# High and low x in one product for three retention projections, memory squares behind a weight cast, and earlier block scores

## The chip, the cores and the metric

The kernel runs on one core of one Trainium2 chip. The metric is device time in microseconds (us) of one execution; the median of three runs of the kernel before is 427.76 us (427.15 to 428.31). Engines are named as in the profile: PE (TensorE matmul), PEld (its weight load), DVE (VectorE), ACT (ScalarE), POOL (GpSimd), SP (SyncE, which issues nearly all transfers).

## The reference

A two-layer decoder trunk over 256 tokens of width 1024, followed by a final norm. Every layer normalises x, projects it to the columns of all its groups, gates each group's output with SiLU, maps the concatenation back with one output projection and adds it to x. Cut to what matters here:

```python
def even_layer(x, mem_n, ...):                      # layer 0
    h = rms_norm(x, norm_g)
    (nq, nkc, ..., mq, mk, mv, mz, eq, ez) = _split(h @ w_in, EVEN_SPLITS)
    a_out = nsa_attention(...)                      # sparse attention, 8 heads; compressed blocks need an MLP
    b_out = moba_attention(rot(mq), rot(mk), heads(mv))        # block attention, 8 heads
    m_out = memory_attention(heads(eq), mem_n, w_mem_kv)       # 4 heads into 256 memory tokens
    y = jnp.concatenate([a_out * silu(nz), b_out * silu(mz), m_out * silu(ez)], -1) @ w_out
    return x + y

def odd_layer(x, mem_n, ...):                       # layer 1
    h = rms_norm(x, norm_g)
    rq, rk, rv, rz, eq, ez = _split(h @ w_in, ODD_SPLITS)      # rq, rk: 4 heads x 256
    q = apply_rotary(rq...); k = apply_rotary(rk...) * (RET_QK_DIM ** -0.5)
    r_out = head_group_norm(retention(q, k, v))     # per head: (q k^T * decay) v + carried state
    m_out = memory_attention(eq..., mem_n, w_mem_kv)
    return x + jnp.concatenate([r_out * silu(rz), m_out * silu(ez)], -1) @ w_out
```

`mem_n` is the memory (256 rows of 1024) normalised by its rows' mean square.

## The kernel before, in words

**Products.** x, memory and every weight are split in two parts, high and low, each in the 32-bit type that the profile calls fp32r. A product is then three matmuls: high x by high weight, low x by high weight, high x by low weight (`mm3`, lines 245 to 247). Weights come in units of 128x1024: SP loads `raw`, ACT makes `whi` (line 166), DVE makes `wlo` = raw - whi (line 174). `whi` and `wlo` have four buffers each (`NB`), so a cast waits until the unit four before it is used up on the PE. A projection of 512 columns takes four units; a unit holds two of the eight row blocks kt for all 512 columns. Where tokens lie on the partitions of the result (`project`), the weight moves (512 columns); where the result is turned, with its 512 columns on partitions in four column tiles ct (`project_turned`), the weight tile is what is loaded and x moves, 256 columns at a time. There each bank of PSUM (128x512) holds two column tiles side by side. The high and low halves of x are two tiles with the tag `big`, four buffers in all; the same tag holds those of the memory, of layer 1's x and the outputs of retention heads 0 and 1.

**Stages.** Layer 0 projects group by group; beside it run the attention chains as generators (`couple`, one for each pair of head pairs): scores on the PE (line 116), maxima (DVE, line 580 causal), exponentials (ACT, line 593), scaling by the gate and the sum (DVE line 555, ACT line 553), transposes on the PE (line 324), copies from PSUM (ACT, line 611), products with the values (PE, line 116), and the SiLU gate (lines 652, 655, 657: `tmp`, then `y` or `ym` as high and low halves). There are four sparse pairs, then block pairs 0 and 1, then the memory attention, which reaches into the out-projection. The rows of the retention projections are called `rq0`, `rk0` (heads 0 and 1) and `rq1`, `rk1` (heads 2 and 3); each is turned, rotated (`ret_qk`, lines 1099 to 1101) and used by two heads.

**What sets the order.** The program is written as stages that yield; each yield of the running projection is a slot, and `turn` then lets every waiting chain do one step (`active`, `first`, `waiting`). `AT` holds slots before which certain steps may not come: "cmp" the compression's rotation and transposes (`compressed`, lines 739 and 740), "blk" its windows, "hid" its hidden layer. A chain takes banks from "s0", "s1", "t", "tr", "o" when they are free; while `crowded` is set, "tr" is not given out. Every engine then runs its instructions in the order in which they were emitted this way (`MANUAL`), SP's transfers included.

**Around the change.** `memory_scale` (generator started after the block values) loads the memory rows (`in_memtok`), squares and sums each row on ACT (line 418), works out the reciprocal root on DVE (`rs`, lines 421 and 132 to 137), and spreads it with two small matmuls (line 879). Its two squares stand between weight casts on ACT, and its DVE steps between the maxima of a sparse pair.

Of the kernel before, what the change touches and what calls it, by code (L numbers as in the profile page):

```python
# [33 lines left out]
AT = {"rows": 4, "rows1": 4, "spread": 12, "ret": 75, "nsa": 12, "cmp": 15, "blk": 18, "hid": 24}  # L34
# [27 lines left out]
def trunk(  # L62
# [165 lines left out]
    def pause(n):  # L228

        for _ in range(n):  # L230
            yield
# [6 lines left out]
    def making(task, *names):  # L238

        yield from task  # L240
        made.update(names)
# [42 lines left out]

    def project_mem(lhs):

        hi, lo = lhs
        ps = [bank("pj") for _ in range(2)]
        for k0 in range(0, KT, 2):
            wh, wl = unit()  # L290
            yield
            turned_unit(ps, lhs, wh, wl, (k0, k0 + 1), range(2))
            finish()
            yield
            for tok in range(2):
                for j in range(2):
                    kt = k0 + j
                    ts = slice(tok * P, (tok + 1) * P)
                    c = slice(j * 512 + 256, j * 512 + 512)
                    mm3(ps[1][:, tok * T : (tok + 1) * T], hi[:, kt, ts], lo[:, kt, ts], wh[:, c], wl[:, c],  # L300
                        kt == 0 and tok == 0, kt == KT - 1, True)
        return ps
# [57 lines left out]
    xh = tl("big", [P, KT, T], 4, F32R)  # L360
    xl = tl("big", [P, KT, T], 4, F32R)
# [195 lines left out]
    def couple(jobs, causal, products, close, name, need=None):  # L557

        spans, cols, blocks = (SPAN, 384, range(3)) if causal else (HALF, 512, (0, 2, 1, 3))
        tags = yield from take(4, FREE)  # L560
# [294 lines left out]
    def memory_rows():  # L855
        nonlocal mh, ml
        mh = tl("big", [P, KT, T], 4, F32R)
        ml = tl("big", [P, KT, T], 4, F32R)
# [9 lines left out]
    def memory_scale():  # L868
# [3 lines left out]
        yield  # L872
        yield from row_scale(mrow, rstdm, D)
        yield
# [52 lines left out]
    def block_couple(c):  # L927
# [4 lines left out]
        def products(o, pts):  # L932
            todo = []
            for i in range(2):
# [6 lines left out]
                          lambda o: making(gated(o, szb, yb, slice(2 * c, 2 * c + 2)), f"Yb{c}"), f"yb{c}")  # L941
# [37 lines left out]
    waiting.extend(({"mq", "mk", "mvt", "szb", f"yb{c - 1}" if c else "yn3"}, block_couple(c)) for c in range(2))  # L979
    drive(memory_queries())  # L980
    crowded = True
    drive(memory_keys())
# [61 lines left out]
    x1h = tl("big", [P, KT, T], 4, F32R)  # L1044
    x1l = tl("big", [P, KT, T], 4, F32R)
# [46 lines left out]
    def ret_qk(name):  # L1092

        both = tl("v4", [P, 2, 2, T], NV)
        ps = now(project_turned((x1h, x1l)))
        for i in range(2):
            pv = ps[i].rearrange("p (k t) -> p k t", k=2)
# [41 lines left out]
    for h in range(4):  # L1139
# [14 lines left out]
        y = tl("big", [P, 2, 4, T], 4, F32R) if h < 2 else tl("y", [P, 2, 4, T], 2, F32R)  # L1154
# [152 lines left out]
```

## Time and profile before

| what | before |
| --- | --- |
| median of 3 runs | 427.76 us (427.15 to 428.31) |
| the profiled execution, its own time | 427.74 us |
| its span | 425.9 us (1.84 us lie around it) |
| granted TensorE clock, mean | 0.999 |
| PE busy | 417.7 us, 98%, 2620 matmuls |
| DVE busy | 305.7 us, 72% |
| ACT busy | 245.6 us, 58% |
| chain that ended last | PE 92%, DVE 3%, DMA 3%, ACT 1% |

The page has one row per engine, groups of instructions by line, and the chain of work that ended last. Matmuls overlap one another, so one that lasts 0.28 us may follow its predecessor by 0.12 us; what counts on a full PE is the distance from start to start. In the rows of the timeline the columns are start, duration (both us), engine, line, operation, output and inputs, shape of the output and count; what stands in brackets is the engine's idle time before the row and what ended it. Line 319 (`rb`) and line 662 (`s<-pj,rstdm`) are copies of 128x256 from PSUM, by DVE and by ACT, in other places of the same kernel.

### The profile page before, as it was taken

To read this page: it belongs to the slowest core of one execution; us is meant where nothing else is said; L and a number is where in the kernel's file an instruction comes from. 1 tells how busy PE (TensorE), PEld (TensorE's weight loads), DVE (VectorE), ACT (ScalarE), POOL (GpSimd) and SP (SyncE) were. 2 spreads that over 40 slices of the span, in tenths; PEclk is the share of its full clock that TensorE was granted. 3 is DMA by queue.
4 is the path that set the end of the run, shared out by engine and by line. 5 is a ranking of instruction groups with operands and counts; after the bars stand their busy time and mean duration, and the time that the engine had idled before them with its cause. 6 is when DMAs were issued, how large, how long until landed. Compare 5 with 4: busy or idle time off the path is not lost.

```text
span 425.9 us, 7020 instructions
## 1 busy us (share of the span) xinstructions
PE 417.7 (98%) x2620; PEld 361.4 (85%) x2620; DVE 305.7 (72%) x675; ACT 245.6 (58%) x453; POOL 1.9 (0%) x9
## 2 busy tenths in 40 slices
PE   8999999999999999999999999999999999999994
PEld 6889987878889887779999988889998888888884
DVE  3878996977678577588578675677887467685545
ACT  4768476777777586755456344456444445545613
POOL 1000000000000000000000000000000000000000
PEclk9999999999999999999999999999999999999999
DMA  7997545254563852536445545546444555656202
GB/s 247 334 372 254 194 136 192 67 184 160 184 191 110 287 175 97 169 128 195 157 145 168 170 167 168 196 159 198 158 158 159 184 192 175 205 170 189 80 0 99
DMA packets 22801, 74.23 MB, mean 174 GB/s; under 512 B 2928, under 2 KB 4464, under 8 KB 22768
## 3 DMA queue, kind: packets, MB, share of 16 engines
q1 hardware_dynamic: 22192, 73.14, 52.2%
q10 hardware_dynamic: 576, 0.66, 0.6%
q8 instruction: 20, 0.33, 0.3%
q14 instruction: 13, 0.11, 0.1%
HBM read 72.73 MB, written 1.05 MB: 173 GB/s over the span
## 4 chain that ended last, share of the span: by engine, by line
PE 92%; DVE 3%; DMA 3%; ACT 1%; issue 0%; SPq 0%; DVEq 0%; ACTq 0%
PE pj L245 23%; PE pj L247 22%; PE pj L246 22%; PE o L116 3%; PE s L409 2%; PE s L324 2%; PE s L116 2%; PE t L324 1%; DMA raw<-in_w 1%; PE tr L245 1%; PE tr L247 1%; PE tr L246 1%; DMA raw<-in_memtok 1%; PE t L116 1%; PE s L246 1%; PE s L247 1%
## 5 line engine op out<-in xcount | busy, mean ns | idle before, releaser
L174 DVE TENSOR_TENSOR wlo<-raw,whi 128x1024 fp32r<-128x1024 f32 (+1 forms) x118 | 142.1, 1207 | 61.8 <-ACT whi L166 59.7
L166 ACT CAST whi<-raw 128x1024 fp32r<-128x1024 f32 (+1 forms) x118 | 121.7, 1036 | 88.4 <-PE pj L247 38.0
L245 PE MATMUL pj<-whi,big 128*128 128x512 f32 (+2 forms) x256 | 97.3, 383 | 0.0
L246 PE MATMUL pj<-wlo,big 128*128 128x512 f32 (+2 forms) x256 | 96.1, 376 | 0.0
L247 PE MATMUL pj<-whi,big 128*128 128x512 f32 (+2 forms) x256 | 95.8, 374 | 0.0
L245 PE MATMUL pj<-big,whi 128*128 128x256 f32 x256 | 73.6, 287 | 0.0
L247 PE MATMUL pj<-big,wlo 128*128 128x256 f32 x256 | 72.6, 284 | 0.0
L246 PE MATMUL pj<-big,whi 128*128 128x256 f32 x256 | 72.5, 283 | 0.0
L245 PEld LDWEIGHTS pj<-whi,big 128*128 128x128 f32 x256 | 48.2, 188 | 9.3 <-issue 1.5
L247 PEld LDWEIGHTS pj<-whi,big 128*128 128x128 f32 x256 | 48.2, 188 | 8.7
L246 PEld LDWEIGHTS pj<-wlo,big 128*128 128x128 f32 x256 | 48.3, 189 | 8.1 <-DVE wlo L174 0.4
L245 PEld LDWEIGHTS pj<-big,whi 128*128 128x128 f32 x256 | 49.0, 191 | 1.9 <-issue 1.8
L246 PEld LDWEIGHTS pj<-big,whi 128*128 128x128 f32 x256 | 49.0, 192 | 0.1
L247 PEld LDWEIGHTS pj<-big,wlo 128*128 128x128 f32 x256 | 49.0, 191 | 0.0
L593 ACT ACTIVATE p<-p,mx 128x128 f32<-128x128 f32 (+1 forms) x48 | 21.2, 443 | 5.3 <-DVE mx L580 5.3
L245 PE MATMUL pj<-whi,y 128*128 128x512 f32 x42 | 16.9, 407 | 0.0
L247 PE MATMUL pj<-whi,y 128*128 128x512 f32 x42 | 16.4, 390 | 0.0
L246 PE MATMUL pj<-wlo,y 128*128 128x512 f32 x42 | 16.3, 391 | 0.0
L555 DVE TENSOR_SCALAR p<-p,sm 128x256 f32<-128x256 f32 (+1 forms) x48 | 12.7, 322 | 0.6
L343 ACT ACTIVATE big<-raw,vec 128x256 fp32r<-128x256 f32 x16 | 7.7, 505 | 5.2 <-DMA vec<-in_vec 2.5
L553 ACT ACTIVATE p<-p,sm 128x256 f32<-128x256 f32 (+1 forms) x16 | 7.6, 484 | 4.9 <-DVE sm L549 4.0
L580 DVE CUSTOM_DVE_ANT_0 p<-s,cst 128x128 f32<-128x128 f32 (+1 forms) x24 | 7.1, 355 | 4.4 <-PE s L116 4.3
(349 smaller groups left out, 644.5 us busy)
## 6 DMA issues: line engine op xcount, KB each, us to landing
raw<-in_w SPq DMA_DIRECT2D x90, 512.0 KB, 3.9
raw<-in_wout SPq DMA_DIRECT2D x28, 512.0 KB, 4.1
v<-in_xtok SPq DMA_DIRECT2D x4, 512.0 KB, 6.4
raw<-in_w SPq DMA_DIRECT2D x4, 280.0 KB, 5.3
raw<-in_w SPq DMA_DIRECT2D x4, 256.0 KB, 6.2
v<-in_w SPq DMA_DIRECT2D x2, 512.0 KB, 7.5
raw<-in_memT SPq DMA_DIRECT2D x2, 512.0 KB, 4.2
raw<-in_memtok SPq DMA_DIRECT2D x2, 512.0 KB, 4.9
```

The source lines that it names most:

```text
L116: ins = PE.matmul(out, lhs, rhs, start=start, stop=stop)
L166: S.copy(hi, raw)
L174: V.tensor_tensor(lo, raw, hi.bitcast(F32), ALU.subtract)
L245: PE.matmul(ps, lh, rh, start=start, stop=False, skip_group_check=shared)
L246: PE.matmul(ps, lh, rl, start=False, stop=False, skip_group_check=shared)
L247: return PE.matmul(ps, ll, rh, start=False, stop=stop, skip_group_check=shared)
L324: PE.transpose(b[:, i * P : (i + 1) * P], a, ident)
L343: S.activation(hi[:, kt], raw[:, kt - k0], AF.Copy, scale=g[:, kt : kt + 1])
L409: PE.matmul(ps_k[tok], x[:, kt, tok * P : (tok + 1) * P], w, start=kt == 0 and i == 0, stop=kt == KT - 1 and i == 2)
L553: S.activation(p[:, hh, a], p[:, hh, a], AF.Copy, scale=sm[:, hh, tok : tok + 1])
L555: V.tensor_scalar(p[:, hh, a], p[:, hh, a], sm[:, hh, tok : tok + 1], None, op0=ALU.mult)
L593: S.activation(ps[i][:, hh, a], src, AF.Exp, bias=ms[i][:, hh, tok : tok + 1], scale=-1.0 if causal else 1.0, accum_out=ns[i][:, hh, tok : ...
```

## The change

Three things are done, and a few steps shift with them.

1. `project_paired` replaces `project_turned` for `rq0`, `rk0` and `rq1`, not for `rk1`. High and low x lie in one tile (`xp`, `mp`, `x1p`: 128 x 2 x 8 x 256), and one matmul moves both, 512 columns, against a high weight tile; a second one moves high x alone, 256 columns, against the low weight tile. The two results of the first stand side by side in a bank, so a projection takes four banks (three "pj" and "tr") where it took two, and `ret_qk` adds the halves: ACT copies the low half to SBUF (line 1119 of the kernel after), DVE adds the high half (line 1120), four times 128x256 each for a projection. The rotation then reads SBUF. `y01` holds the outputs of heads 0 and 1 in one tile, so that all uses of `big` have the new size (two buffers).
2. `memory_scale` waits two slots before the squares and three before the spread.
3. The block pairs no longer wait for the gate path `szb`; block pair 1 may take "tr", "s0", "s1", "t" for its scores; `crowded` is set only after the memory keys. "cmp" is 14 instead of 15 and "hid" 23 instead of 24.

The diff (in the kernel after, lines of `couple` and the rest of layer 0 stand 17 further down: 418 becomes 435, 555 becomes 572, 580 becomes 597, 611 becomes 628; those of `ret_qk` 25):

```diff
@@ -31,7 +31,7 @@
 BANKS = {"pj": 3, "tr": 1, "t": 1, "s0": 1, "s1": 1, "o": 1}
 FREE = ("s0", "s1", "t", "tr", "o")
 NEG = -1e30
-AT = {"rows": 4, "rows1": 4, "spread": 12, "ret": 75, "nsa": 12, "cmp": 15, "blk": 18, "hid": 24}
+AT = {"rows": 4, "rows1": 4, "spread": 12, "ret": 75, "nsa": 12, "cmp": 14, "blk": 18, "hid": 23}
 MAGIC = 12582912.0
 PI_LO = 3.1415925
 BASE = 16512 + 32 + 416 + 32
@@ -282,6 +282,23 @@
                 finish()
         return ps
 
+    def project_paired(pair):
+
+        ps = [bank(tag) for tag in ("pj", "pj", "pj", "tr")]
+        for kt in range(0, KT, 2):
+            wh, wl = unit()
+            for ct in range(4):
+                if ct % 2 == 0:
+                    yield
+                for j in range(2):
+                    c = slice(j * 512 + ct * P, j * 512 + ct * P + P)
+                    k = kt + j
+                    PE.matmul(ps[ct], wh[:, c], pair[:, :, k], start=k == 0, stop=False, skip_group_check=True)
+                    PE.matmul(ps[ct][:, :T], wl[:, c], pair[:, 0, k], start=False, stop=k == KT - 1, skip_group_check=True)
+                if ct % 2:
+                    finish()
+        return ps
+
     def project_mem(lhs):
 
         hi, lo = lhs
@@ -357,8 +374,8 @@
     G.memset(warm, 0.0)
     ident = cpak[:, C_ID : C_ID + P]
     xrow = [tl("v4", [P, D], NV) for _ in range(2)]
-    xh = tl("big", [P, KT, T], 4, F32R)
-    xl = tl("big", [P, KT, T], 4, F32R)
+    xp = tl("big", [P, 2, KT, T], 2, F32R)
+    xh, xl = xp[:, 0], xp[:, 1]
     ps_k = [bank(f"s{tok}") for tok in range(2)]
     xraw, wraw = [], []
     for q in range(4):
@@ -554,10 +571,10 @@
                 else:
                     V.tensor_scalar(p[:, hh, a], p[:, hh, a], sm[:, hh, tok : tok + 1], None, op0=ALU.mult)
 
-    def couple(jobs, causal, products, close, name, need=None):
+    def couple(jobs, causal, products, close, name, need=None, banks=FREE):
 
         spans, cols, blocks = (SPAN, 384, range(3)) if causal else (HALF, 512, (0, 2, 1, 3))
-        tags = yield from take(4, FREE)
+        tags = yield from take(4, banks)
         ss, todo = [], []
         for i, (q, k, gate) in enumerate(jobs):
             ss.append([bank(tag) for tag in tags[2 * i : 2 * i + 2]])
@@ -854,8 +871,8 @@
 
     def memory_rows():
         nonlocal mh, ml
-        mh = tl("big", [P, KT, T], 4, F32R)
-        ml = tl("big", [P, KT, T], 4, F32R)
+        mp = tl("big", [P, 2, KT, T], 2, F32R)
+        mh, ml = mp[:, 0], mp[:, 1]
         for q in range(2):
             mraw = load(tl("raw", [P, 1024], NRAW), memT[:, 4 * q : 4 * q + 4].rearrange("p k t -> p (k t)")).rearrange("p (k t) -> p k t", k=4)
             yield
@@ -869,9 +886,9 @@
         nonlocal rstdm, rbm
         mrow = [load(tl("raw", [P, 1024], NRAW), memtok[:, tok]) for tok in range(2)]
         rstdm = tl("rstdm", [P, 2])
-        yield
+        yield from pause(2)
         yield from row_scale(mrow, rstdm, D)
-        yield
+        yield from pause(3)
         rbm = tl("rbm", [P, T])
         tag, = yield from take()
         b = bank(tag)
@@ -938,7 +955,8 @@
             return todo
 
         yield from couple([(mq[:, 2 * c + i], mk[:, 2 * c + i], None) for i in range(2)], True, products,
-                          lambda o: making(gated(o, szb, yb, slice(2 * c, 2 * c + 2)), f"Yb{c}"), f"yb{c}")
+                          lambda o: making(gated(o, szb, yb, slice(2 * c, 2 * c + 2)), f"Yb{c}"), f"yb{c}",
+                          banks=("tr", "s0", "s1", "t") if c else FREE)
 
     def memory_keys1():
         nonlocal k1, v1m
@@ -976,10 +994,10 @@
     drive(block_values())
     active.append(making(memory_scale(), "rbm"))
     drive(block_gates())
-    waiting.extend(({"mq", "mk", "mvt", "szb", f"yb{c - 1}" if c else "yn3"}, block_couple(c)) for c in range(2))
+    waiting.extend(({"mq", "mk", "mvt", f"yb{c - 1}" if c else "yn3"}, block_couple(c)) for c in range(2))
     drive(memory_queries())
+    drive(memory_keys())
     crowded = True
-    drive(memory_keys())
 
 
     def part(acc, tok, c0, n, y, k, wh, wl, start, stop):
@@ -1041,8 +1059,8 @@
     strict = crowded = False
 
 
-    x1h = tl("big", [P, KT, T], 4, F32R)
-    x1l = tl("big", [P, KT, T], 4, F32R)
+    x1p = tl("big", [P, 2, KT, T], 2, F32R)
+    x1h, x1l = x1p[:, 0], x1p[:, 1]
     ss1 = tl("ss1", [P, 2, 2])
     rstd1 = tl("rstd1", [P, 2])
     rb1 = tl("rb", [P, T], 2)
@@ -1092,9 +1110,16 @@
     def ret_qk(name):
 
         both = tl("v4", [P, 2, 2, T], NV)
-        ps = now(project_turned((x1h, x1l)))
+        paired = name != "rk1"
+        ps = now(project_paired(x1p) if paired else project_turned((x1h, x1l)))
         for i in range(2):
-            pv = ps[i].rearrange("p (k t) -> p k t", k=2)
+            if paired:
+                pv = tl("rot_a", [P, 512], 2).rearrange("p (k t) -> p k t", k=2)
+                for k in range(2):
+                    S.copy(pv[:, k], ps[2 * i + k][:, T:])
+                    V.tensor_tensor(pv[:, k], ps[2 * i + k][:, :T], pv[:, k], ALU.add)
+            else:
+                pv = ps[i].rearrange("p (k t) -> p k t", k=2)
             b = tl("rot_b", [P, 512]).rearrange("p (k t) -> p k t", k=2)
             V.tensor_tensor(both[:, i], pv, ctr.unsqueeze(1).to_broadcast([P, 2, T]), ALU.mult)
             V.tensor_tensor(b, pv[:, ::-1, :], str_, ALU.mult)
@@ -1151,7 +1176,9 @@
         sz = tl("v4", [P, 2, 512], NV)
         for tok in range(2):
             S.activation(sz[:, tok], ps[tok], AF.Silu, scale=rstd1[:, tok : tok + 1])
-        y = tl("big", [P, 2, 4, T], 4, F32R) if h < 2 else tl("y", [P, 2, 4, T], 2, F32R)
+        if h == 0:
+            y01 = tl("big", [P, 2, 2, 4, T], 2, F32R)
+        y = y01[:, h] if h < 2 else tl("y", [P, 2, 4, T], 2, F32R)
         ret_head(h, qs[h % 2], kks[h % 2], vh, vl, sz, y)
         ys.append((y, 4, 6 + 2 * h, ()))
```

How instructions move, as each engine runs them (names carry the number under which their tile was made; `s` names are banks "s0", "s1" or SBUF tiles of the tag `s2`, `t`, `tr`, `o`, `pj` are banks).

ACT, around the squares of the memory rows, before (`raw_1257` and `raw_1259` are the memory rows, `whi` the weight casts, `pt` the copies of sparse pair 1's transposes, `y` and `p` the gate and exponentials behind):

```order
L611 COPY pt_1275<-o_1250 128x384
L418 ACTIVATE raw_1257,ss_1278<-raw_1257 128x1024
L166 CAST whi_1292<-raw_1083 128x1024
L418 ACTIVATE raw_1259,ss_1278<-raw_1259 128x1024
L166 CAST whi_1363<-raw_1141 128x1024
L655 CAST y_82<-tmp_275_1334 128x256
L593 ACTIVATE p_1336,sm_1338<-p_1336,mx_1337 128x128
```

and after:

```order
L628 COPY pt_1273<-o_1248 128x384
L166 CAST whi_1288<-raw_1081 128x1024
L435 ACTIVATE raw_1255,ss_1316<-raw_1255 128x1024
L435 ACTIVATE raw_1257,ss_1316<-raw_1257 128x1024
L166 CAST whi_1353<-raw_1139 128x1024
L672 CAST y_81<-tmp_273_1331 128x256
L610 ACTIVATE p_1333,sm_1335<-p_1333,mx_1334 128x128
```

The first weight cast now stands ahead of the first square, and the second one behind both. The six DVE steps of `rs` that follow the squares (lines 421 and 132 to 137) stood between the maxima of a sparse pair's two halves, and now stand behind both halves, ahead of the same `wlo` (line 174).

PE, the scores of block pair 1 (`v_173` are the keys and `v_210` the queries, in the kernel after `v_172` and `v_209`; `v_251` there are the values and `pt` the turned probabilities; the other rows are the memory keys' projection). Before, they stand alone between two units' matmuls, while the products of block pair 0 stand 24 matmuls ahead of them:

```order
L245 MATMUL pj_1677<-big_1058,whi_1679 128x256
L246 MATMUL pj_1677<-big_1059,whi_1679 128x256
L247 MATMUL pj_1677<-big_1058,wlo_1680 128x256
L116 MATMUL s_349_1796<-v_173_859,v_210_1033 128x128
L116 MATMUL s_350_1797<-v_173_859,v_210_1033 128x128
L116 MATMUL s_349_1796<-v_173_859,v_210_1033 128x256
L116 MATMUL s_350_1797<-v_173_859,v_210_1033 128x256
L116 MATMUL t_1798<-v_173_859,v_210_1033 128x128
L116 MATMUL o_1799<-v_173_859,v_210_1033 128x128
L116 MATMUL t_1798<-v_173_859,v_210_1033 128x256
L116 MATMUL o_1799<-v_173_859,v_210_1033 128x256
L245 MATMUL pj_1678<-whi_1679,big_1058 128x256
```

After, they follow the products of block pair 0 at once:

```order
L116 MATMUL o_1738<-pt_1690,v_251_1233 64x128 x2
L116 MATMUL o_1738<-pt_1717,v_251_1233 64x256 x2
L116 MATMUL o_1738<-pt_1717,v_251_1233 64x128 x2
L116 MATMUL tr_1747<-v_172_858,v_209_1032 128x128
L116 MATMUL s_344_1748<-v_172_858,v_209_1032 128x128
L116 MATMUL tr_1747<-v_172_858,v_209_1032 128x256
L116 MATMUL s_344_1748<-v_172_858,v_209_1032 128x256
L116 MATMUL s_345_1749<-v_172_858,v_209_1032 128x128
L116 MATMUL t_1750<-v_172_858,v_209_1032 128x128
L116 MATMUL s_345_1749<-v_172_858,v_209_1032 128x256
L116 MATMUL t_1750<-v_172_858,v_209_1032 128x256
L245 MATMUL pj_1683<-big_1057,whi_1638 128x256
```

One interruption of the projection remains of two. The same holds for the scores of block pair 0 and the products of sparse pair 3. What follows is earlier too: in the out-projection, the products of the memory attention stood 6 matmuls ahead of the first matmul that reads `ym`, and now stand 24 ahead of it.

PE, `rq0`, beginning behind scores of the memory attention, before (`big_2205` is high x, `big_2206` low x):

```order
L116 MATMUL t_2540<-s_462_2403,s_478_2530 128x256
L116 MATMUL tr_2541<-s_462_2403,s_478_2530 128x256
L245 MATMUL pj_2619<-big_2205,whi_2470 128x256
L246 MATMUL pj_2619<-big_2206,whi_2470 128x256
L247 MATMUL pj_2619<-big_2205,wlo_2471 128x256
```

and after, from the last column tile of `rq0` (bank `tr_2618`) to the first of `rk0` (banks `pj_2726` to `pj_2728`; `big_2203` holds both halves of x):

```order
L297 MATMUL tr_2618<-big_2203,wlo_2642 128x256
L296 MATMUL tr_2618<-big_2203,whi_2641 128x512
L296 MATMUL pj_2726<-big_2203,whi_2663 128x512
L296 MATMUL pj_2727<-big_2203,whi_2663 128x512
L296 MATMUL pj_2728<-big_2203,whi_2663 128x512
L297 MATMUL pj_2726<-big_2203,wlo_2664 128x256
```

A group of three matmuls over 256 columns became one over 512 and one over 256. The column tile that uses "tr" is left to the end of the projection in all four units, 16 matmuls in a row, of which the first two rows show two (a third, like the first of them, is left out behind them), since the memory attention, or the column tile "tr" of the projection before, still holds that bank; the next projection's first weight half can be cast only when the first of these units has been used there, and three matmuls by high weights stand ahead of the first by a low one.

## The prediction

> **What bounds the kernel now.** I read the page first, then a table of busy time by stretches, then the PE's list of waits.
>
> ```profile
> span 425.9 us, 7020 instructions
> PE 417.7 (98%) x2620; PEld 361.4 (85%) x2620; DVE 305.7 (72%) x675; ACT 245.6 (58%) x453; POOL 1.9 (0%) x9
> PE 92%; DVE 3%; DMA 3%; ACT 1%; issue 0%; SPq 0%; DVEq 0%; ACTq 0%
> ```
>
> The PE is busy for 98% of the span and carries 92% of the chain that ended last. A change pays only if it takes work, or a wait, off the PE. The stretches (PE, PEld, DVE, ACT, POOL busy, clock, DMA share, GB/s) tell where a wait is:
>
> ```profile
> 110.00:120.00 10.00, 8.84 (x73) 8.39 (x72) 9.55 (x43) 8.61 (x25) 0.00 (x0) 1.00 0.67 207
> 210.00:220.00 10.00, 10.00 (x84) 9.40 (x83) 7.08 (x9) 3.44 (x6) 0.00 (x0) 1.00 0.64 211
> 230.00:240.00 10.00, 10.00 (x86) 9.26 (x83) 8.11 (x11) 3.67 (x4) 0.00 (x0) 1.00 0.56 181
> ```
>
> At 110 to 120 us, in layer 0, the PE lacks 1.16 us while DVE is nearly full; at 210 to 240, where `rq0` and `rk0` are projected, it lacks nothing. The list of waits and the PE's own rows name the hole:
>
> ```profile
> PE s L324 <- DVE p L555: 1.2, 1, 1.2
> 115.86 0.28 PE L247 MATMUL pj<-big,wlo 128*128 128x256 f32 x1
> 117.29 0.92 PE L324 MATMUL s<-cst,p 128*128 128x128 f32 x5 [1.16 <-DVE p L555]
> ```
>
> From start to start this is 1.43 us where 0.12 is usual (below): 1.3 us are lost. The rows of ACT and DVE ahead of it say why:
>
> ```profile
> 107.71 1.06 ACT L418 ACTIVATE raw<-raw 128x1024 f32<-128x1024 f32 x1 [3.62 <-DMA raw<-in_memtok]
> 108.77 1.03 ACT L166 CAST whi<-raw 128x1024 fp32r<-128x1024 f32 x1
> 109.70 1.05 ACT L418 ACTIVATE raw<-raw 128x1024 f32<-128x1024 f32 x1
> 112.00 0.40 ACT L593 ACTIVATE p<-p,mx 128x128 f32<-128x128 f32 x1
> 109.83 1.23 DVE L174 TENSOR_TENSOR wlo<-raw,whi 128x1024 fp32r<-128x1024 f32 x1 [5.49 <-ACT whi L166]
> 110.97 0.42 DVE L652 TENSOR_TENSOR tmp<-o,v 128x256 f32<-128x256 f32 x1
> 112.41 0.17 DVE L421 TENSOR_SCALAR ss<-ss 128x2 f32<-128x2 f32 x1
> 113.41 0.16 DVE L137 SCALAR_TENSOR_TENSOR rstdm<-rs_t,rstdm 128x2 f32<-128x2 f32 x1
> 115.07 1.23 DVE L174 TENSOR_TENSOR wlo<-raw,whi 128x1024 fp32r<-128x1024 f32 x1
> 116.95 0.74 DVE L555 TENSOR_SCALAR p<-p,sm 128x128 f32<-128x128 f32 x3
> ```
>
> ACT sits for 3.62 us on a square whose memory rows have not landed; a weight cast is queued behind it; DVE idles 5.49 us for that cast and then has no pause until the probabilities `p` that the PE waits for.
>
> **The change, part by part.**
>
> *Memory squares behind the cast: −1.3 us.* The cast no longer needs the memory rows, so it runs inside ACT's 3.62 us, near 104.1 (107.71 less 3.62), its `wlo` and the first `tmp` before 107, and the maxima as their scores come. The rows still land at 107.7, so two squares end at about 109.75 (107.71 plus twice 1.0) and the second cast at 110.8, one cast (1.03) earlier than before relative to the exponentials: these start at about 111.0 rather than 112.00. The DVE steps on the squares take 1.2 us (112.41 to 113.41 and one more step), so they end at 111.0; the second `wlo` follows. From that `wlo` to the first `p` it was 1.88 us (115.07 to 116.95) and to the PE 2.22, so the PE could go at about 113.3.
>
> The last of the four blocks of `p` is scaled by ACT, behind all eight exponentials:
>
> ```profile
> L593 ACT ACTIVATE p<-p,mx 128x128 f32<-128x128 f32 (+1 forms) x48 | 21.2, 443 | 5.3 <-DVE mx L580 5.3
> L553 ACT ACTIVATE p<-p,sm 128x256 f32<-128x256 f32 (+1 forms) x16 | 7.6, 484 | 4.9 <-DVE sm L549 4.0
> ```
>
> 111.0 + 8 x 0.443 + 0.484 = 115.0. The PE arrives at 115.98 (115.86 + 0.12), or some tenths earlier by what is saved ahead. The cover is about 0.7 us, so I take the whole 1.3. If the squares held the exponentials as the cast did, nothing would be gained; so the bounds are 0 and −1.3. The spread behind them moves too, to a place beside no other work on the PE; its four DVE rows have been ready for long, and it costs a mode change (below).
>
> *Pairing: −1.15 us.* First and last rows of two even stretches, 75 steps of 256 columns and 11 of 512:
>
> ```profile
> 208.09 0.28 PE L245 MATMUL pj<-big,whi 128*128 128x256 f32 x1
> 217.09 0.28 PE L245 MATMUL pj<-big,whi 128*128 128x256 f32 x1
> 263.68 0.39 PE L245 MATMUL pj<-whi,big 128*128 128x512 f32 x1
> 266.18 0.39 PE L247 MATMUL pj<-whi,big 128*128 128x512 f32 x1
> ```
>
> That is 0.120 us for 256 columns and 0.227 for 512; so a matmul costs 0.013 us beside its columns (2 x 0.120 − 0.227). Each group drops one of them: 3 x 0.120 = 0.360 becomes 0.347. There are 3 projections x 32 groups = 96: 96 x 0.012 = 1.15 us off the path. No row alternates 512 and 256. Should the 0.013 sit in the weight load rather than in the matmul, the alternation would hide it wholly (0.107 for 256 columns and 0.214 for 512, 0.321 a group, −3.8 us in all); should a 512 behind a 256 pay for it twice, nothing would be saved (0). I take the constant, since 512 columns, with ample time for a load, show it as well.
>
> By the Trainium skill, "TensorE: Matmul & The Clock Gate", section "Back-to-back issue gap", a warm matmul takes 262 cycles for 256 columns and 518 for 512; my estimate from that page is 786 against 780 cycles a group, 0.24 us in all. The trace's 0.120 us is more than the 0.109 of 262 cycles at the page's 2.4 GHz, and 0.227 more than 0.216; the measured rows decide, and a sum by the page would end 0.9 us higher.
>
> *The additions of the halves: 0 to +0.6, taken as 0.1.* Per projection, four ACT copies and four DVE additions, and the rotation's six rows as before:
>
> ```profile
> L662 ACT ACTIVATE s<-pj,rstdm 128x256 f32<-128x256 f32 x4 | 1.7, 463 | 1.8 <-PE pj L247 1.8
> L1099 DVE TENSOR_TENSOR v<-pj,ctr 128x512 f32<-128x512 f32 x8 | 5.5, 683 | 0.0
> L174 DVE TENSOR_TENSOR wlo<-raw,whi 128x1024 fp32r<-128x1024 f32 (+1 forms) x118 | 142.1, 1207 | 61.8 <-ACT whi L166 59.7
> ```
>
> ACT gets 4 x 0.46 = 1.9 us more in 11 us and is below 4 in 10 there. DVE has 4 x 1.21 + 6 x 0.68 = 8.9, plus 4 x 0.42 (the price of `tmp` at 110.97) = 10.6 of the 32 x 0.347 = 11.1 us that the PE takes. It fits with half a microsecond to spare. The closer point is the step from `rq0` to `rk0` and from there to `rv0`: the weight buffers are held until the column tile in "tr" begins. From the end of the second 512 by the first unit (row 1225 of the PE) to the first matmul by the next low half lie six groups (6 x 0.347), three by high weights (3 x 0.227) and the second 256 of that unit (0.12): 2.88 us from start to start, 2.72 when the 0.16 is taken off by which a 512 outlasts its successor's start (0.39 − 0.227). Cast and `wlo` need 1.03 + 1.23, and their handoffs about 0.2: 2.46. It is covered by 0.26 us. Should DVE be 0.5 late at both, it is +0.5; I take 0.1.
>
> *Fewer interruptions: −0.5 us.* Changing between the projection's matmuls and the attention's costs PE time at both ends:
>
> ```profile
> 105.08 0.28 PE L247 MATMUL pj<-big,wlo 128*128 128x256 f32 x1
> 105.29 1.52 PE L116 MATMUL o<-pt,s 128*64 128x256 f32 x16
> 108.68 0.39 PE L245 MATMUL pj<-big,whi 128*128 128x256 f32 x1
> 108.91 0.28 PE L246 MATMUL pj<-big,whi 128*128 128x256 f32 x1
> ```
>
> 0.21 and 0.23 where 0.12 is usual, so 0.2 for a round trip. By the order there are 23 such trips where there were 26, and one fewer into transposes: −0.6 at most. If scores directly behind products cost half of it again, −0.3; I take −0.5.
>
> *Earlier gating of the memory attention: −0.4 us.* The start of the out-projection's last part:
>
> ```profile
> 183.50 0.50 PE L245 MATMUL pj<-whi,ym 128*128 128x512 f32 x1
> 183.84 0.40 PE L246 MATMUL pj<-wlo,ym 128*128 128x512 f32 x1
> 184.23 0.50 PE L247 MATMUL pj<-whi,ym 128*128 128x512 f32 x1
> 184.56 0.40 PE L245 MATMUL pj<-whi,ym 128*128 128x512 f32 x1
> 183.48 0.69 DVE L657 TENSOR_TENSOR ym<-tmp,ym 128x512 fp32r<-128x512 f32 x1 [0.69 <-ACT ym L655]
> ```
>
> Three steps of 0.34, 0.39 and 0.33 stand where 0.227 is usual: 0.38 us, while DVE still writes `ym` until 184.17. With its products 18 matmuls (4.1 us) earlier, `ym` is ready long before. In layer 1 the products of the memory attention come closer to the copies of its transposes on ACT, which now also holds two copies of the halves (0.46 each); four such copies
>
> ```profile
> 226.92 0.66 ACT L611 COPY pt<-tr 128x512 f32<-128x512 f32 x1
> ```
>
> at 0.48 a step have a PE cover of some 2.2 us against 2.4: +0.2.
>
> *The compression a slot earlier: 0.* Its transposes move 12 matmuls forward:
>
> ```profile
> 37.79 0.27 PE L739 MATMUL o<-cst,rot_a 128*128 128x128 f32 x1
> 35.73 0.37 ACT L732 ACTIVATE tmp<-t,rstd 128x128 f32<-128x128 f32 x1 [0.50 <-DVE gates L728]
> ```
>
> from 37.79 to 36.35, and ACT is done at 36.10. Covered by 0.25; if the slot's work comes later, up to +0.3.
>
> **The sum.** −1.3 − 1.15 + 0.1 − 0.5 − 0.4 + 0.2 = −3.05 against the profiled execution's 427.74 (425.9 and 1.84 around it; the median is 427.76, so it stands for it): 424.7 us. A measurement of this kernel tells about 0.3%, 1.28 us, from no change.
>
> **The rivals.**
> - *The stall stays.* The memory rows land no earlier, and now both squares stand ahead of the cast and the exponentials. If they hold these as long as the cast did, the PE waits its 1.3 us: 426.0. Against it: 0.7 us of cover. 12 in 100.
> - *Pairing saves nothing*, because the 512 behind a 256 pays for its longer run, or since its x comes from two places: 424.7 + 1.15 = 425.9. No row excludes it. 13 in 100. The page's small floor, named above, would lead to almost this time.
> - *DVE or ACT lags in the paired stretches* by about 0.5 us in each of three projections: 426.2. For it: 10.6 of 11.1 us. 9 in 100.
> - *Slower: weights late at both edges.* If a cast and its `wlo` start only when the tile in "tr" has ended, for instance because DVE is still rotating, 2.46 us are exposed for each, or 4.9 in all: 429.6. It decides when DVE or ACT is more than 0.26 us late there, and ends above the time before only when over 1.5 us are exposed at both. 5 in 100.
> - *Pairing hides the whole constant:* 424.7 − 2.65 = 422.1. 8 in 100.
> - The forecast has 53 in 100.
>
> **The numbers.** The predicted time is that of the forecast, 424.7. The range goes from 423.2 (half of the constant hidden beside) to 426.6 (one of the first three rivals in full, with a little beside it); it leaves out the slower case, the fast one, and two of the first three together, about 2 in 10. Faster by over 0.3% means below 426.48: the forecast, the fast rival and most of the first three, 0.83. Within 0.3%: 0.12, from two of the first three together. Slower: 0.05.
>
> **What would show it.** Right: no wait on `p` near 116 us, ACT casting a weight before the first square of `in_memtok`; groups of 0.347 us in `rq0`, `rk0` and `rq1`; `ym` matmuls at 0.23 from the start; the first low matmul of `rk0` without a wait. Wrong: a wait of the PE on `wlo` at the start of `rk0` or `rv0`, a group at 0.36, or a DVE that goes without a pause through `rq0`.

## The result and the profile after

The changed kernel takes 425.01 us (median of 4 runs, 424.92 to 425.05), the one before 427.45 us (4 runs, 427.0 to 428.31): a ratio of 0.9934, interval 0.9915 to 0.9953. The prediction was 424.7, from 423.2 to 426.6. The profiled execution took 425.04 us, 2.70 less than the one before.

The head of the page, the PE's list of waits, and its stretches (as above):

```profile
span 423.3 us, 6853 instructions
PE 415.4 (98%) x2524; PEld 355.7 (84%) x2524; DVE 309.7 (73%) x687; ACT 249.6 (59%) x465; POOL 1.9 (0%) x9
PE 92%; DMA 3%; DVE 3%; ACT 1%; issue 1%; SPq 0%; DVEq 0%; ACTq 0%
```

```profile
PE t L417 <- POOL kcbd L733: 1.3, 1, 1.3
PE s L426 <- ACT whi L144: 0.4, 1, 0.4
PE pj L246 <- DVE wlo L174: 0.3, 1, 0.3
```

```profile
110.00:120.00 10.00, 10.00 (x87) 10.00 (x86) 8.60 (x35) 9.88 (x30) 0.00 (x0) 1.00 0.52 172
210.00:220.00 10.00, 10.00 (x68) 8.60 (x68) 7.89 (x13) 6.78 (x19) 0.00 (x0) 1.00 0.55 194
230.00:240.00 10.00, 10.00 (x58) 8.73 (x57) 8.44 (x14) 4.32 (x8) 0.00 (x0) 1.00 0.69 211
```

The 96 matmuls are gone, the PE fills 110 to 120 us, and the wait on `p` is no longer in the list. Its last two entries stand at 8.46 and 28.12 us, in the start of the execution (see the yardstick below), and not at the edges that the prediction named. The squares and the PE at that place (ACT first):

```profile
104.64 1.06 ACT L166 CAST whi<-raw 128x1024 fp32r<-128x1024 f32 x1
109.07 1.06 ACT L435 ACTIVATE raw<-raw 128x1024 f32<-128x1024 f32 x1 [3.37 <-DVE mx L597]
110.34 1.06 ACT L435 ACTIVATE raw<-raw 128x1024 f32<-128x1024 f32 x1
111.39 1.03 ACT L166 CAST whi<-raw 128x1024 fp32r<-128x1024 f32 x1
116.50 0.28 PE L247 MATMUL pj<-big,wlo 128*128 128x256 f32 x1
116.62 0.82 PE L341 MATMUL s<-cst,p 128*128 128x128 f32 x6
```

The cast runs inside ACT's idle time, as foretold, and the PE goes from the projection to the transposes in 0.12 us. The squares began 1.36 us later than in the kernel before (0.7 of it behind the first sparse pair's products, the rest the later start), and still nothing waits.

The matmuls that read `ym`:

```profile
181.72 0.39 PE L245 MATMUL pj<-whi,ym 128*128 128x512 f32 x1
181.94 0.39 PE L246 MATMUL pj<-wlo,ym 128*128 128x512 f32 x1
182.17 0.39 PE L247 MATMUL pj<-whi,ym 128*128 128x512 f32 x1
```

They follow at 0.22 to 0.23 us, where before it was 0.33 to 0.39. In the paired projection I show the first and the ninth 512 of an even stretch (8 groups), the step to the memory attention's products, and the two edges, `rq0` to `rk0` and `rk0` to `rv0`:

```profile
217.29 0.40 PE L296 MATMUL pj<-big,whi 128*128 128x512 f32 x1
...
220.12 0.40 PE L296 MATMUL pj<-big,whi 128*128 128x512 f32 x1
...
224.58 0.28 PE L297 MATMUL pj<-big,wlo 128*128 128x256 f32 x1
224.94 1.95 PE L116 MATMUL o<-pt,s 128*64 128x256 f32 x16
...
229.74 0.88 PE L296 MATMUL pj<-big,whi 128*128 128x512 f32 x3
230.45 0.28 PE L297 MATMUL pj<-big,wlo 128*128 128x256 f32 x1
...
240.97 0.63 PE L245 MATMUL pj<-whi,big 128*128 128x512 f32 x2
241.43 0.40 PE L246 MATMUL pj<-wlo,big 128*128 128x512 f32 x1
```

A group takes 2.83 / 8 = 0.354 us, where I had 0.347. Over all of them a 512 between two 256s takes 0.2356 on the mean of 75, and a 256 between two 512s 0.1169 of 70: 0.3525. The products wait about 0.15 us (0.36 less 0.12 and 0.09 for the change of kind), for ACT's last copy of transposes, which ended at 224.89. At the edges the first low matmul comes three and two steps of 0.23 to 0.24 behind the first high one: no wait.

**A yardstick.** The start of an execution is uneven: the weights of the first units land at different times. So executions are compared from the first sparse pair's products to the last transposes. In the kernels before and after:

```profile
71.51 0.65 PE L116 MATMUL o<-pt,s 128*64 128x256 f32 x4
394.78 0.49 PE L324 MATMUL t<-cst,tmp 128*128 128x128 f32 x3
```

```profile
72.15 0.65 PE L116 MATMUL o<-pt,s 128*64 128x256 f32 x4
392.08 0.49 PE L341 MATMUL t<-cst,tmp 128*128 128x128 f32 x3
```

From start to start that is 323.27 us before and 319.93 after, −3.34; the start of this execution came 0.64 later. I cut the stretch at two more places: at the transposes of `p` that waited (117.29 before) and at the spread of layer 1's norm (line 317):

```profile
206.09 0.27 PE L317 MATMUL tr<-cst,rstd 128*128 128x128 f32 x1
```

The table has these lengths, read the same way from one profiled execution of each kernel. In kernels with the block part the spread stands four matmuls of 256 columns earlier, so 0.48 us is moved there from the last column to the one ahead.

| kernel | first products at | to transposes of p | to the spread | to the last transposes | all |
| --- | --- | --- | --- | --- | --- |
| before | 71.51 | 45.78 | 88.80 | 188.69 | 323.27 |
| after | 72.15 | 44.47 | 87.25 | 188.21 | 319.93 |
| e1 pairing alone | 71.79 | 46.18 | 88.82 | 188.20 | 323.20 |
| e2 squares alone | 71.83 | 44.46 | 89.53 | 188.68 | 322.67 |
| e3 block part alone | 71.33 | 46.12 | 87.62 | 188.68 | 322.42 |
| e4 slots alone | 72.18 | 46.44 | 88.84 | 188.68 | 323.96 |
| e5 squares and block part | 71.76 | 44.47 | 87.25 | 188.69 | 320.41 |
| e6 halves side by side | 71.79 | 44.47 | 87.26 | 188.20 | 319.93 |
| e7 high, high, low, low | 71.13 | 44.46 | 87.26 | 188.09 | 319.81 |
| e8 rk1 paired too | 71.58 | 44.47 | 87.25 | 189.29 | 321.01 |
| e9 the changed kernel again | 71.62 | 44.47 | 87.25 | 188.21 | 319.93 |
| e10 rotation behind low | 71.72 | 44.47 | 87.25 | 188.16 | 319.88 |

Where nothing was edited, these lengths repeat to 0.04 us, while the times of whole runs scatter by half a microsecond and more. The exception is the first column of the four kernels that still wait on `p` (before, e1, e3, e4): it runs from 45.78 to 46.44, since the memory rows land at different times. The readings below rest on the table first.

### The profile page after: what moved, and what is told of

Its sections match the earlier page's. It is cut to its first block, busy times and chain, and to the rows that moved or that the text cites. A ratio compares the mean times of both kernels' runs of the same rounds, so it can differ in the third digit from the quotient of the medians.

```text
span 423.3 us, 6853 instructions
## 1 busy us (share of the span) xinstructions
PE 415.4 (98%) x2524; PEld 355.7 (84%) x2524; DVE 309.7 (73%) x687; ACT 249.6 (59%) x465; POOL 1.9 (0%) x9
## 4 chain that ended last, share of the span: by engine, by line
PE 92%; DMA 3%; DVE 3%; ACT 1%; issue 1%; SPq 0%; DVEq 0%; ACTq 0%
PE pj L245 21%; PE pj L246 20%; PE pj L247 20%; PE pj L296 4%; PE o L116 4%; DMA raw<-in_w 3%; PE s L341 2%; PE pj L297 2%; PE s L116 2%; PE t L341 2%; PE tr L296 1%; PE tr L247 1%; PE tr L246 1%; PE tr L245 1%; PE t L116 1%; PE s L426 1%
## 5 line engine op out<-in xcount | busy, mean ns | idle before, releaser
L245 PE MATMUL pj<-big,whi 128*128 128x256 f32 x160 | 46.0, 288 | 0.0
L246 PE MATMUL pj<-big,whi 128*128 128x256 f32 x160 | 45.4, 284 | 0.0
L247 PE MATMUL pj<-big,wlo 128*128 128x256 f32 x160 | 45.3, 283 | 0.0
L245 PEld LDWEIGHTS pj<-big,whi 128*128 128x128 f32 x160 | 30.6, 191 | 1.1 <-issue 1.0
L246 PEld LDWEIGHTS pj<-big,whi 128*128 128x128 f32 x160 | 30.6, 191 | 0.0
L247 PEld LDWEIGHTS pj<-big,wlo 128*128 128x128 f32 x160 | 30.6, 191 | 0.0
L296 PE MATMUL pj<-big,whi 128*128 128x512 f32 x72 | 25.6, 402 | 0.0
L297 PE MATMUL pj<-big,wlo 128*128 128x256 f32 x72 | 19.0, 282 | 0.0
L296 PEld LDWEIGHTS pj<-big,whi 128*128 128x128 f32 x72 | 13.3, 188 | 2.8 <-issue 0.3
L297 PEld LDWEIGHTS pj<-big,wlo 128*128 128x128 f32 x72 | 13.6, 189 | 0.6
```

What stands on the lines that cost most here:

```text
L245: PE.matmul(ps, lh, rh, start=start, stop=False, skip_group_check=shared)
L246: PE.matmul(ps, lh, rl, start=False, stop=False, skip_group_check=shared)
L247: return PE.matmul(ps, ll, rh, start=False, stop=stop, skip_group_check=shared)
L296: PE.matmul(ps[ct], wh[:, c], pair[:, :, k], start=k == 0, stop=False, skip_group_check=True)
L297: PE.matmul(ps[ct][:, :T], wl[:, c], pair[:, 0, k], start=False, stop=k == KT - 1, skip_group_check=True)
```

## Experiments

**Each part alone.** Four kernels, each the kernel before with one part of the change.

e1, pairing:

```diff
+    xp = tl("big", [P, 2, KT, T], 2, F32R)          # likewise mp, x1p, y01
+        ps = now(project_paired(x1p) if paired else project_turned((x1h, x1l)))
```

> The kernel before with the pairing of rq0, rk0 and rq1 alone (high and low x in one tile, additions in ret_qk). The prediction's step says -1.15 us and +0.3 for what comes with it. My theory after the trace of the changed kernel: a group takes 0.354 us and not 0.347, so 96 groups save 0.6, and the memory attention's products in layer 1 give 0.15 to 0.3 of it back: -0.3 to -0.5 us against the kernel before, 0.999. Rival: the late start of layer 0 seen there (weights of the first units 0.6 us late) belongs to the larger tiles; then +0.2 us. In its trace the PE reaches rq0 when the kernel before does, unless the rival holds.

Measured: 427.82 us against 428.38, ratio 0.9987 (0.9974 to 1.0001), not clear by itself. Over the yardstick −0.07: layer 1 gained 0.49 (188.69 to 188.20) and the wait on `p` grew by 0.40. The theory's −0.3 to −0.5 holds for the part that was edited. The growth has nothing to do with pairing, since layer 0 has the same instructions: the list of the PE's waits and ACT's rows show

```profile
PE s L341 <- DVE p L572: 1.6, 1, 1.6
108.40 1.06 ACT L435 ACTIVATE raw<-raw 128x1024 f32<-128x1024 f32 x1 [4.16 <-DMA raw<-in_memtok]
```

that is, the memory rows landed later in this execution, and so the PE waited 1.6 us. Its start (71.79) is not later than in e2, e4 and e5 (71.83, 72.18 and 71.76), which lack the larger tiles; that speaks against the rival.

e2, squares:

```diff
-        yield
+        yield from pause(2)
         yield from row_scale(mrow, rstdm, D)
-        yield
+        yield from pause(3)
```

> The kernel before with the two longer pauses of the memory squares alone. Theory: the wait of 1.2 us on p near 116 us goes and nothing follows, -1.3 to -1.7 us, 0.9965. Rival: without the earlier block scores or the spread at its new place something else waits (the spread stands alone beside the projection and the memory keys come up behind it): -0.5 us or nothing.

Measured: 427.65 us against 428.38, ratio 0.9984 (0.9974 to 0.9994); over the yardstick −0.60. The rival holds. The wait on `p` went (45.78 to 44.46), and a new one came, here from the list and from the PE's rows:

```profile
PE pj L245 <- ACT ym L655: 1.4, 1, 1.4
179.86 1.95 PE L116 MATMUL o<-pt,s 128*64 128x256 f32 x16
183.25 0.50 PE L245 MATMUL pj<-whi,ym 128*128 128x512 f32 x1 [1.44 <-ACT ym L655]
```

The later pauses set the memory keys' chain back by a step, and the products of the memory attention now stand directly ahead of the first matmul that reads `ym` (6 matmuls lay between them before). Of the 1.32 us that the squares gained at 117 us, the gate takes back 0.73 at 183, by which the next column grew.

e3, the block pairs:

```diff
-    waiting.extend(({"mq", "mk", "mvt", "szb", f"yb{c - 1}" if c else "yn3"}, block_couple(c)) for c in range(2))
+    waiting.extend(({"mq", "mk", "mvt", f"yb{c - 1}" if c else "yn3"}, block_couple(c)) for c in range(2))
...
-    crowded = True
     drive(memory_keys())
+    crowded = True
```

(and the banks of block pair 1)

> The kernel before with the block pairs' part alone (no wait for the gate path, banks of pair 1, crowded later). Theory: two merged interruptions at 0.2 and ym without a wait (0.4), -0.7 to -0.9 us, 0.998. Rival: the merged interruptions bring nothing by themselves (only ym counts): -0.4 us. The wait on p near 116 us is expected to stay, 1.2 us.

Measured: 427.26 us, ratio 0.9979 (0.9961 to 0.9997); −0.85 over the yardstick, of which −1.18 in the middle column and +0.34 in a longer wait on `p`:

```profile
PE s L324 <- DVE p L555: 1.5, 1, 1.5
```

So this part is worth more than two merged interruptions and `ym` (0.8) had made me expect. The PE's steps in that column tell from what. It has five round trips to the attention's matmuls where it had seven (0.40), and nothing is lost at the first matmuls that read `ym` (0.41). And the eight transposes of `p` for the memory attention, which before were held by ACT's scaling of one block, run without a stop (0.22), here before and in e3:

```profile
173.90 1.25 PE L324 MATMUL s<-cst,p 128*128 128x128 f32 x8
169.50 1.03 PE L324 MATMUL s<-cst,p 128*128 128x128 f32 x8
```

That makes 1.03 of the 1.18; the rest is spread over 512s that follow one another at 0.233 to 0.247 and not at 0.227, of which there are 27 before and 11 in e3.

e4, the slots:

```diff
-AT = {..., "cmp": 15, "blk": 18, "hid": 24}
+AT = {..., "cmp": 14, "blk": 18, "hid": 23}
```

> The kernel before with the two slots of the compression alone (14 and 23). Theory: one more and one fewer change between kinds of matmul, 0.0 +- 0.2 us. Rival: the part of layer 0 ahead of 60 us, which ran 0.6 us later in the changed kernel, is slower by this edit: +0.6 us. If the lateness is there in kernels whose first 29 us are the same instruction by instruction, it is the arrival of the weights and no edit's.

Measured: 428.85 us, ratio 1.0011 (0.9995 to 1.0026): no difference. Over the yardstick +0.69, all of it the wait on `p`, the longest of the lot:

```profile
PE s L324 <- DVE p L555: 1.8, 1, 1.8
109.05 1.06 ACT L418 ACTIVATE raw<-raw 128x1024 f32<-128x1024 f32 x1 [3.99 <-DMA raw<-in_memtok]
```

The rest changed by +0.03. Its first products came at 72.18, like those of the changed kernel; but up to 29 us its instructions and transfers are the same as before's, one by one, and the kernel e9, which has the same slots, had them at 71.62. The lateness is the arrival of weights: in e4 the PE waits 0.87 us at 9.06 us for a cast, and ACT had waited 1.71 us for that weight's transfer.

**The two that need one another.** e5 has the edits of e2 and e3 together, without pairing and slots.

> The kernel before with the memory squares' pauses and the block pairs' part, without pairing and without the two slots. From the first sparse pair's products (71.5 us) to the last transposes, the squares alone gained 0.60 us and the block part alone 0.85. Theory: they need one another, since the squares alone bring the memory attention's products next to the matmuls that read ym (a wait of 1.4 us), which the earlier block scores undo, and the block part alone leaves the wait on p; together -2.7 to -2.9 us over that stretch, time 0.9935, and no wait on p or ym. Rival: the two add up, -1.5 us.

Measured: 425.46 us against 427.65, ratio 0.9948 (0.9934 to 0.9963); −2.86 over the yardstick, where e2 and e3 alone add to −1.45. The theory holds. The PE's whole list of waits is one line, at the very start:

```profile
PE t L400 <- POOL kcbd L716: 1.3, 1, 1.3
```

With e1's −0.49 and e4's 0.03 this gives −3.3, the changed kernel's −3.34: nothing is left unexplained at this level.

**Why a group saves less than forecast.** e6 keeps the instructions and their order and lays the halves of each row block side by side, so that the 512 columns are one run.

```diff
-    x1p = tl("big", [P, 2, KT, T], 2, F32R)
-    x1h, x1l = x1p[:, 0], x1p[:, 1]
+    x1p = tl("big", [P, KT, 2, T], 2, F32R)
+    x1h, x1l = x1p[:, :, 0], x1p[:, :, 1]
...
-                    PE.matmul(ps[ct], wh[:, c], pair[:, :, k], ...)
+                    PE.matmul(ps[ct], wh[:, c], pair[:, k], ...)
```

> The changed kernel with high and low x of a row block next to each other (128 x 8 x 2 x 256), so that the 512 columns which a paired matmul moves are one run; same instructions in the same order. In the changed kernel a paired 512 takes 0.235 us and not the 0.227 of the other 512s. Theory: that is the price of two runs that lie 2048 elements apart; then 0.227 here, 0.345 a group, and -0.7 us against the changed kernel. Rival: it is the price of the change of length or weights; then 0.235 as before and the same time.

Measured: 424.53 us against 427.65, ratio 0.9923 (0.9907 to 0.994); over the yardstick exactly the changed kernel's 319.93. The rival holds: a 512 between 256s takes 0.2354 (75 of them). The first and the ninth 512 of the stretch shown above are here

```profile
217.30 0.40 PE L296 MATMUL pj<-big,whi 128*128 128x512 f32 x1
...
220.12 0.40 PE L296 MATMUL pj<-big,whi 128*128 128x512 f32 x1
```

2.82 / 8 = 0.353 us a group: the two runs of the moved operand cost nothing.

e7 issues, per column tile and unit, both matmuls by high weights and then both by low ones.

```diff
-                for j in range(2):                       # 512, 256, 512, 256
-                    PE.matmul(ps[ct], wh[:, c], pair[:, :, k], ...)
-                    PE.matmul(ps[ct][:, :T], wl[:, c], pair[:, 0, k], ...)
+                for low in range(2):                     # 512, 512, 256, 256
+                    for j in range(2):
+                        ...
```

> The changed kernel with the matmuls of two row blocks in another order: both by high weights (512, 512), then both by low ones (256, 256); the length changes half as often. Theory that the two runs cost (see the run with halves side by side): 512 stays at 0.235 here, same time. Rival, that going between 512 and 256 costs: half the excess goes, 0.231 for a 512, -0.4 us against the changed kernel.

Measured: 424.5 us against 427.65, ratio 0.9924 (0.9909 to 0.9939). A stretch of three double groups:

```profile
217.63 0.62 PE L300 MATMUL pj<-big,whi 128*128 128x512 f32 x2
218.09 0.40 PE L298 MATMUL pj<-big,wlo 128*128 128x256 f32 x2
...
219.72 0.63 PE L300 MATMUL pj<-big,whi 128*128 128x512 f32 x2
```

2.09 / 6 = 0.348 us a group, close to the 0.347 of the forecast. So the rival holds in kind: a good part of the excess belongs to the change between 512 and 256 columns, and goes when the changes are halved. The weights, which change between high and low as well, are no rival for it: in the even stretches of the prediction they change too, at 0.120 and 0.227. But the excess does not end with the first matmul after a change. Where six 512s follow 256s in e7 (from 230.57 us), their steps are 0.233, 0.236, 0.228, 0.233, 0.230 and 0.227. What inside the PE makes it so stays open. At 0.349 on the mean 96 groups should save 0.34, and the yardstick shows 0.12; most of the rest is lost at one edge, `rk0` to `rv0` (PE, then DVE):

```profile
239.65 0.63 PE L245 MATMUL pj<-whi,big 128*128 128x512 f32 x2
240.27 0.50 PE L246 MATMUL pj<-wlo,big 128*128 128x512 f32 x1
237.78 0.69 DVE L1127 TENSOR_TENSOR v<-rot_a,ctr 128x512 f32<-128x512 f32 x1
238.39 0.68 DVE L1128 TENSOR_TENSOR rot_b<-rot_a,str 128x512 f32<-128x512 f32 x1
238.99 1.22 DVE L174 TENSOR_TENSOR wlo<-raw,whi 128x1024 fp32r<-128x1024 f32 x1
```

The first low matmul comes 0.62 us behind the first high one, where two steps are 0.46: the PE waits 0.16 for a `wlo` that stands behind two instructions of `rk0`'s rotation. In the changed kernel the same `wlo` was done 0.25 us ahead of its matmul. The step behind it takes 0.34 and not 0.23, another 0.11. This is the edge of the prediction's slower rival: behind the first sparse pair's products the PE comes to it 0.30 us earlier than in the changed kernel (168.52 against 168.82), the `wlo` 0.06 later, and that is enough to reach it.

**Pairing the fourth projection.** e8:

```diff
-        paired = name != "rk1"
+        paired = True
```

> The changed kernel with rk1 paired too, so that all four are. From the group's measured 0.353 us where three matmuls take 0.360, 32 groups save 0.24 us if the additions (4 x 0.46 on ACT, 4 x 0.42 on DVE) and the bank held for the tile in tr hide: -0.2 us. Rival: DVE, which normalises heads 0 and 1 and rotates rq1 there (9.5 of 10 us busy at 300 to 310), delays weights or q and k of head 2: +0.3 to +1.5 us with a wait of the PE on wlo.

Measured: 425.88 us against 427.65, ratio 0.9961 (0.9946 to 0.9977); +1.08 over the changed kernel's yardstick, all of it in layer 1. The rival's time holds, though not its reason: the PE waits for the addition of the halves, which must read a bank before the next projection may use it.

```profile
PE pj L245 <- DVE rot_a L1120: 1.1, 1, 1.1
312.50 3.50 DVE L174 TENSOR_TENSOR wlo<-raw,whi 128x1024 fp32r<-128x1024 f32 x3 [2.34 <-ACT whi L166]
315.91 1.08 DVE L1120 TENSOR_TENSOR rot_a<-pj,rot_a 128x256 f32<-128x256 f32 x3
```

DVE was not short of time there: it idled 2.34 us for a cast, which itself waited for the column tile in "tr" to begin, and then made three `wlo` in a row ahead of the additions.

**The changed kernel again, and the edge taken away.** e9 is the changed kernel itself.

> The changed kernel itself once more, beside the next one and with more runs of the kernel before. Theory: -3.3 us from the first sparse pair's products (71 to 72 us) to the last transposes, as in its first trace, while the time up to those products differs from execution to execution by up to 0.9 us for the same instructions; time 0.993. Rival: the start belongs to the kernel: then the products come at 72.1 again and not at 71.1 to 71.8.

Measured: 424.68 us against 428.21, ratio 0.9912 (0.9895 to 0.993). Every column of the table repeats, and the first products came at 71.62: the theory holds.

e10 is e7 with the first instruction of `rk0`'s rotation, in both its halves, made to wait for `rv0`'s first `wlo`.

```diff
+            low = ready[0][1]                            # rv0's first low half
+            for _ in range(3):                           # three steps of rv0's projection
+                slot[0] += 1
+                next(stage)
+            rotated(kb, pvs, lows[id(low)])
...
+            if behind is not None:
+                after(ins, behind)
```

> The kernel with high, high, low, low in a paired projection (e7), and the rotation of rk0 made to wait for the first low weight half of rv0. In e7 the first low matmul of rv0 came 0.16 us late, since DVE rotated rk0 ahead of that half; the grouping saved 0.34 us by its groups and 0.12 in all. Theory: the lateness goes, -0.15 to -0.3 us against e7, 0.3 to 0.4 against the changed kernel over the stretch from the first sparse products to the last transposes. Rival: the lateness comes from ACT's casts or the buffers, then nothing changes; or k of head 0, rotated later, makes the PE wait at the scores of head 0, +0.2.

Measured: 424.32 us against 428.21, ratio 0.9905 (0.9886 to 0.9923), not to be told from e9 (424.07 to 425.02, against 424.2 to 424.57). The lateness at the edge went:

```profile
240.24 0.63 PE L246 MATMUL pj<-whi,big 128*128 128x512 f32 x2
240.71 0.39 PE L247 MATMUL pj<-wlo,big 128*128 128x512 f32 x1
```

0.47 for two steps. Over the yardstick it is 0.07 worse than e7 all the same. The order of emission, which the part on the kernel gives for the whole program, holds for layer 0 only: the kernel closes it there (`order.close()`), and in layer 1 instructions stand in another order than they are emitted (the three first matmuls of `rk0`, `pj_2726` to `pj_2728`, are emitted with matmuls by low weights between them). With one dependence more the scores of head 0 and `rq1` came out in another order too, so that what else changed can't be told apart here. None of e6, e7 and e10 is faster than the changed kernel by more than the measurement is uncertain.

## Why the prediction was right or wrong

- **The sum.** −3.05 was forecast against the profiled execution. Over the yardstick it is −3.34; this execution's start came 0.64 late, which gives the −2.70 between the two profiles. The start was no step of mine, and I had taken a difference of two executions for one of two kernels. That the sum came this close is partly luck: the middle column gained 1.55 where interruptions and `ym` were to bring 0.9, layer 1 gained 0.48 where pairing and what it costs were to bring 0.85, and the late start took 0.64.
- **Squares, −1.3.** Right in mechanism and size (45.78 to 44.47), but not a gain of its own: alone it brings 0.60 (e2), because the pauses also move the memory attention onto `ym`. I had gone through what the pauses release and not through who waits for the chain that they delay; it is the block part of the same change that undoes it. The 0.7 us of cover was mis-sized. I had both memory rows landing at 107.7; in the trace before they landed at 107.63 and 109.10, and in all twelve the second came 1.2 to 2.1 us behind the first. The second square can wait for it, as in e7:

```profile
108.32 1.06 ACT L438 ACTIVATE raw<-raw 128x1024 f32<-128x1024 f32 x1 [0.90 <-DMA raw<-in_memtok]
```

After the change the rows landed at 108.98 and 110.25, and ACT's block of `p` was done at 116.66, when the PE had already begun the others at 116.62; it loads this one fifth, at 116.95. So 0.29 us of cover was left, the least of the eight traces with the later squares: by that, rows that land another 0.3 us later would have brought a wait back.
- **Pairing, −1.15.** Mis-sized. The constant of 0.013 us a matmul is right for equal matmuls in a row; between 512 and 256 a step costs about 0.006 more per group. By groups it is 96 x 0.0075 = 0.72. With the wait of 0.15 at the memory attention's products (forecast 0.2) and what else comes with it, e1 has 0.49 and the changed kernel beside e5 0.48. The rivals with nothing (0) and with the whole constant hidden (−3.8) both fail. The Trainium skill, "TensorE: Matmul & The Clock Gate", section "Back-to-back issue gap", would give 6 cycles a group, an estimate of 0.24 us in all; the measured 0.72 by groups lies between that and my forecast, and the rows decide.
- **Interruptions and `ym`, −0.5 and −0.4.** Near for what they name (0.40 and 0.41 in e3's steps), but the column gained −1.18 for the block part alone, and −1.55 with the squares. What I left out are transposes held by blocks of `p`: 0.22 at 174 us by a block that ACT scales, which the block part takes away, and about 0.2 behind the wait at 117 us, where before five transposes took 0.92 us, the second held by DVE's next block (done at 117.50), and six take 0.82 now. With the squares the spread also stands apart from these transposes (some 0.16).
- **Slots, 0.** Right: 0.03 beside a wait that belongs to the memory rows.
- **The slower rival** did not come, at a distance of 0.25 us at the `rv0` edge (the forecast said 0.26); e7 and e8 show both sides of it, a `wlo` behind a rotation and a bank behind an addition.

## What to carry to other kernels

A wait taken away early in a full engine's time is only a gain if everything that the edit delays is still covered where it is read: follow the delayed chain to its last reader, and try the edit alone and together with its partner. Compare two executions from the first point that both reach undisturbed, and part by part; the whole times here scatter by more than any part is worth. Merging two equal matmuls into a longer one saves less when it leaves matmuls of two lengths taking turns, and the additions that it needs have to be priced at the place where a bank or a weight buffer is handed on.

## What the hardware showed beside

- The first products came at 71.13 to 72.18 us in the twelve traces, whose instructions differ up to there in the two slots alone, and the changed kernel had them at 72.15 and at 71.62. The first memory row landed at 106.19 to 108.98 us. Where the PE waited on `p`, the wait followed the rows: the first square began at 107.71, 107.88, 108.40 and 109.05 us, 36.20, 36.55, 36.61 and 36.87 behind the first products, and the wait was 1.2, 1.5, 1.6 and 1.8 us.
- A 512-column matmul is followed after 0.227 us by another, after 0.2356 when 256-column ones stand on both sides, and the 256 is followed after 0.117 instead of 0.120; whether its 512 columns are one run or two makes no difference (0.2354).
